# A two-block network in fp32 on one core: hi|lo products of the second MLP and of the SwiGLU side by side, and the order of the work changed in the attention, three norm boundaries and the gates

## The chip, the cores and the metric

The kernel runs on one core of a Trainium2 chip. The metric is the device time of one launch in microseconds (us). The kernel before takes 940.36 us (median of 3 runs, 940.02 to 941.78).

## The reference

256 tokens with 1024 features pass through two residual blocks, a final norm, and then a third block of another kind. All weights and activations are fp32. What matters here:

```python
for i in range(2):                       # first_block
    mod = silu(c) @ w_mod[i] + b_mod[i]
    sh1, sc1, g1, sh2, sc2, g2 = split(mod, 6)
    h = rmsnorm(x, norm_mix[i]) * (1 + sc1) + sh1
    y = pool_mixer(h) if i == 0 else moba_attention(h)
    x = x + g1 * y
    h = rmsnorm(x, norm_mlp[i]) * (1 + sc2) + sh2
    x = x + g2 * (relu(h @ w_up[i]) ** 2 @ w_down[i])   # w_up 1024 x 4096
...
h = concat(meta, rmsnorm(x, norm_final))  # second_block, 16 meta tokens ahead
proj = rmsnorm(h) @ w_in                  # gated deltanet + forgetting attention
h = h + concat(o_gdn, o_fox) @ w_out
f = rmsnorm(h)
h = h + (silu(f @ w_gate) * (f @ w_up)) @ w_down        # hidden width 2816
```

With 256 tokens the MoBA attention has a single key block: it is causal attention of 16 heads of 64 features with a relative-position bias.

## The kernel before, in words

**Products.** Every fp32 number that enters a matmul is held as two fp32r parts, hi (the rounded value) and lo (the rest). `mm3` (L261) makes one product out of three matmuls: hi·hi (L262), and the two mixed ones (L263, L264). A weight arrives in pieces of 128x1024 by DMA (queue of SP), its hi half is made on ACT (`piece_hi`, L245) and its lo half on DVE (`piece_lo`, L251); five such pairs can stand at once. With the weights stationary (`ws_steps`, L959) one tile of 128 output features and 256 tokens takes 8 k-steps of `mm3`, so 24 matmuls of 256 columns; with the tokens stationary (`tm_steps`, L970) the columns are 512 features.

**MLP and SwiGLU.** `mlp` (L1034) runs over 8 chunks of 512 hidden features. `up` (L1072) makes the four feature tiles of a chunk in two pairs, each pair in one PSUM bank of 512 columns; `split_act` (L1086) squares the relu and splits it into hi and lo for `dn`, the product with w_down (48 matmuls of 512 columns per chunk). Chunk 0 of MLP 1 (`up_first`, L1058) is made with tokens stationary and then transposed (`upt`), one half of the tokens after the other; it is followed by chunk 1's `up` and chunk 0's `dn`. In the SwiGLU `gate_up` (L1998, ten times) and `swi` (L1974) do the like for a chunk of 256 hidden features, with silu(gate) times up; the product with w_down there is `fd`.

**PSUM.** Eight banks: four for accumulators (`acc_tile`), two for products (`mm_tile`) and two for transposes (`tp_tile`).

**Boundaries.** `boundary` (L521) stands between a block half and the next: it adds the gated result to x (DVE), squares and sums (ACT), takes the reciprocal root (DVE), normalizes (`normalize`, L547), transposes on PE (8 matmuls per half of the tokens, `*_tp`), scales by the modulation (`scaled`, ACT) and splits into hi and lo (`split`, DVE, L395 and L396). Its order on ACT, DVE and PE is as written. Between the two token halves PE works on what is held back: `products(n)` takes n steps from the generator `ahead`, which are the previous section's last products (two `mm3`, six matmuls each) and, in two boundaries, then the next section's first products of 128 tokens. Boundary att1 leads into the attention, mlp1 into MLP 1, f into the SwiGLU. In mlp1 `R_HOLD` = 3 such steps come before the first transposes.

**Attention.** `attention` (L1138) writes PE's order by hand: a clock of estimated costs runs along the projections (`project`, `quarter_values`, `wo`), and a table of events with due times (`H_S`, `H_P`, `H_T`, `H_V` and so on) places, for each pair of heads, the scores, the softmax (`softmax_rows`, DVE L1115 to L1120 and ACT L1118), the transposes of P (`pt`) and the product P·V (`pv`). After each projection and each quarter of the values `riding` (L1182) lets one unit of another job go: two columns of the modulation (`wmc`, L444), that is a DMA of 1024 KB on SP and two row products of 128x1024 on DVE. There are ten such places, and the first six use the job up.

**Gates.** In the second block `interleave` (L111) mixes the deltanet's convolution products (`conv_proj`) with the gates' short chain (`early_gates`); `R_GATE` is how many steps of the chain follow each step of the products.

Everything else is ordered by the tile framework's scheduler. The few lines of the arithmetic that the change replaces:

```python
def mm3(ps, l, r, first, last):
    pe.matmul(ps, l[0], r[0], start=first, stop=False)
    pe.matmul(ps, l[0], r[1], start=False, stop=False)
    pe.matmul(ps, l[1], r[0], start=False, stop=last)
```

Of the kernel before, what the change touches and what calls it, by code (L numbers as in the profile page):

```python
# [36 lines left out]
R_GATE = 2.0  # L37
# [4 lines left out]
H_V = 2.0  # L42
H_TL = 5.0
DELAY = 3
C_FEAT = 0.6
# [5 lines left out]
R_HOLD = 3  # L51
# [59 lines left out]
def interleave(main, filler, ratio=None):  # L111

    owed = 0.0
    for r in main:
        owed += r if ratio is None else ratio
# [42 lines left out]
def build(tc, a, out):  # L158
# [4 lines left out]
    with ctx:  # L163
# [357 lines left out]
        def boundary(ac, gate, scale, shift, h, c0, name, ahead, final=None):  # L521
# [3 lines left out]
            with tc.manual_schedule(engines=VA | {mybir.EngineType.PE}):  # L525
# [80 lines left out]
                elif w is not None:  # L606
# [3 lines left out]
                    products(8)  # L610
# [8 lines left out]
                    w.piece_lo(3)  # L619
                    normalize(1)  # L620
                else:
# [347 lines left out]

        def tm_steps(w, h, tok0, m, ps, grain=2):  # L970
# [63 lines left out]
        def mlp(i, h, w0, wn, at, ahead=None):  # L1034


            def act2(src, name):
                n = src.shape[1]
                r = t2k(f"{name}r")[:, :n]
# [32 lines left out]
            def up(j):  # L1072
                w = ahead if i == 0 and j == NUP else split_chunk(a[f"w_up_{i}"][j - (1, NUP)[i == 0]], f"wu{i}{j}")
                ab = a_tile(j)
                for pr in range(2):
                    ps = mm_tile(f"up{i}{j}{pr}")
                    for q in range(2):
                        weights_stationary(w, h, 2 * pr + q, ps[:, q * S:(q + 1) * S])
# [59 lines left out]
        def attention(i, h, w0, wn):  # L1138
# [7 lines left out]
            st = {}  # L1146

# [34 lines left out]
            def riding():  # L1182
                ride(4)
# [158 lines left out]
        h = boundary(ac, lambda: gates[1, 0], *mods(1, 1), hl_tiles("mlp1", S), 0, "mlp1", (rest, wu1))  # L1342
# [783 lines left out]
```

## Time and profile before

| | |
|---|---|
| median of 3 runs | 940.36 us (940.02 to 941.78) |
| the profiled execution | 940.04 us |
| its span (first to last instruction) | 938.3 us |
| PE busy | 910.2 us (97%), 6045 matmuls |
| DVE busy | 638.0 us (68%) |
| ACT busy | 497.7 us (53%) |
| POOL busy | 12.5 us (1%) |
| DMA | 198.31 MB, mean 211 GB/s |
| mean granted PE clock | 0.995 |

The profile is that of one execution. PE is the engine of the matmuls, DVE the vector engine, ACT the scalar engine, POOL GpSimd, SP the engine that issues the DMAs. Matmuls overlap each other, so that one matmul's duration in a row is longer than the time from its start to the next one's start; the latter is called the cadence here and is what counts. A bracket behind a row gives the time for which the engine stood idle before it, and what released it.

### The profile page before, as it was taken

How to read it: one execution, taken by the hardware profiler on the slowest of the kernel's cores; microseconds unless marked ns; L12 is line 12 of the kernel's file. 1: busy time of each engine (PE TensorE's matmuls, PEld its weight loads, DVE VectorE, ACT ScalarE, POOL GpSimd, SP SyncE). 2: the span in 40 equal slices, each digit the busy share in tenths (PEclk: the TensorE clock that was granted, in tenths of full speed). 3: DMA queues.
4: the chain of work that ended last, by engine and by line, in shares of the span. 5: the costliest groups of instructions: out<-in, count | busy, mean ns of one | idle time of the engine just before them, and what ended most of it. 6: DMA issues, size and time to landing. Idle time of an engine off the chain costs nothing.

```text
span 938.3 us, 15294 instructions
## 1 busy us (share of the span) xinstructions
PE 910.2 (97%) x6045; PEld 794.0 (85%) x6045; DVE 638.0 (68%) x1222; ACT 497.7 (53%) x881; POOL 12.5 (1%) x22
## 2 busy tenths in 40 slices
PE   6999999999998999999999999999999999999996
PEld 3668889988797977889999978899988799999995
DVE  1686898878797775875556667797558765555544
ACT  4476444445556663744455555766456554444442
POOL 0000000000000000000000001000000000000000
PEclk9999999999999999999999999999999999999999
DMA  9998899889285560875565545332112555555531
GB/s 364 420 420 316 317 358 353 340 320 342 93 331 197 169 225 0 299 274 180 197 221 180 198 152 169 121 120 92 46 46 91 201 195 198 187 184 180 180 136 45
DMA packets 34555, 198.31 MB, mean 211 GB/s; under 512 B 4186, under 2 KB 6818, under 8 KB 14002
## 3 DMA queue, kind: packets, MB, share of 16 engines
q1 hardware_dynamic: 34338, 197.27, 59.0%
q8 instruction: 47, 0.77, 0.3%
q14 instruction: 24, 0.20, 0.1%
q10 hardware_dynamic: 146, 0.08, 0.0%
HBM read 196.24 MB, written 1.09 MB: 210 GB/s over the span
## 4 chain that ended last, share of the span: by engine, by line
PE 87%; DVE 5%; DMA 3%; ACT 2%; issue 2%; POOL 0%; DVEq 0%; POOLq 0%; ACTq 0%
PE up L262 7%; PE up L264 6%; PE up L263 6%; PE dn L262 6%; PE dn L264 6%; PE dn L263 6%; PE gu L264 4%; PE gu L263 4%; PE gu L262 4%; PE qk L291 2%; PE fd L262 2%; PE fd L263 2%; PE fd L264 2%; PE cp L264 1%; PE cp L262 1%
## 5 line engine op out<-in xcount | busy, mean ns | idle before, releaser
L262 PE MATMUL up<-mlp_hi,wu_h 128*128 128x256 f32 x416 | 118.5, 285 | 0.0
L264 PE MATMUL up<-mlp_hi,wu_l 128*128 128x256 f32 x416 | 117.7, 283 | 0.6 <-DVE wu_l L251 0.6
L263 PE MATMUL up<-mlp_lo,wu_h 128*128 128x256 f32 x416 | 117.9, 284 | 0.0
L245 ACT ACTIVATE wd_h<-wd_r 128x1024 fp32r<-128x1024 f32 x58 | 61.3, 1060 | 66.2 <-PE up L263 42.1
L245 ACT ACTIVATE wu_h<-wu_r 128x1024 fp32r<-128x1024 f32 x58 | 60.8, 1063 | 65.9 <-PE dn L264 48.8
L251 DVE TENSOR_TENSOR wu_l<-wu_r,wu_h 128x1024 fp32r<-128x1024 f32 x58 | 70.3, 1221 | 36.9 <-ACT wu_h L245 36.6
L251 DVE TENSOR_TENSOR wd_l<-wd_r,wd_h 128x1024 fp32r<-128x1024 f32 x58 | 70.7, 1222 | 35.4 <-ACT wd_h L245 34.9
L262 PE MATMUL dn<-wd_h,a 128*128 128x512 f32 x232 | 91.1, 393 | 0.0
L263 PE MATMUL dn<-wd_l,a 128*128 128x512 f32 x232 | 90.9, 392 | 0.0
L262 PE MATMUL gu<-f_hi,wgu_h 128*128 128x256 f32 x320 | 90.7, 283 | 0.0
L264 PE MATMUL gu<-f_hi,wgu_l 128*128 128x256 f32 x320 | 90.6, 283 | 0.0
L263 PE MATMUL gu<-f_lo,wgu_h 128*128 128x256 f32 x320 | 90.6, 283 | 0.0
L264 PE MATMUL dn<-wd_h,a 128*128 128x512 f32 x232 | 90.4, 390 | 0.0
L251 DVE TENSOR_TENSOR wgu_l<-wgu_r,wgu_h 128x1024 fp32r<-128x1024 f32 x44 | 53.6, 1224 | 51.3 <-ACT wgu_h L245 51.3
L262 PEld LDWEIGHTS up<-mlp_hi,wu_h 128*128 128x128 f32 x416 | 79.7, 192 | 1.0 <-issue 0.5
L263 PEld LDWEIGHTS up<-mlp_lo,wu_h 128*128 128x128 f32 x416 | 79.7, 192 | 1.0 <-issue 0.5
L264 PEld LDWEIGHTS up<-mlp_hi,wu_l 128*128 128x128 f32 x416 | 79.7, 192 | 0.8 <-DVE wu_l L251 0.8
L245 ACT ACTIVATE wgu_h<-wgu_r 128x1024 fp32r<-128x1024 f32 x44 | 46.6, 1062 | 62.0 <-PE gu L263 29.4
L263 PEld LDWEIGHTS gu<-f_lo,wgu_h 128*128 128x128 f32 x320 | 61.4, 192 | 0.3
L262 PEld LDWEIGHTS gu<-f_hi,wgu_h 128*128 128x128 f32 x320 | 61.4, 192 | 0.4
L264 PEld LDWEIGHTS gu<-f_hi,wgu_l 128*128 128x128 f32 x320 | 61.4, 192 | 0.0
L264 PEld LDWEIGHTS dn<-wd_h,a 128*128 128x128 f32 x232 | 43.6, 188 | 10.0 <-issue 0.9
(792 smaller groups left out, 2269.7 us busy)
## 6 DMA issues: line engine op xcount, KB each, us to landing
wu_r<-in_w_up_dram SPq DMA_DIRECT2D x32, 1024.0 KB, 5.2
wd_r<-in_w_down_dram SPq DMA_DIRECT2D x32, 1024.0 KB, 6.4
wgu_r<-in_w_gu_dram SPq DMA_DIRECT2D x22, 1024.0 KB, 5.2
wmc<-in_w_modc_dram SPq DMA_DIRECT2D x16, 1024.0 KB, 6.9
wmg<-in_w_modg_dram SPq DMA_DIRECT2D x12, 1024.0 KB, 6.8
wfd_r<-in_w_fd_dram SPq DMA_DIRECT2D x11, 1024.0 KB, 4.8
wi_r<-in_w_in_dram SPq DMA_DIRECT2D x10, 1024.0 KB, 5.1
wms<-in_w_mods_dram SPq DMA_DIRECT2D x16, 512.0 KB, 9.9
```

Of the source, the lines that this page charges most:

```text
L245: act.activation(hi, r, AF.Copy)
L251: vec.tensor_tensor(lo, r, hi.bitcast(F32), ALU.subtract)
L262: pe.matmul(ps, l[0], r[0], start=first, stop=False)
L263: pe.matmul(ps, l[0], r[1], start=False, stop=False)
L264: pe.matmul(ps, l[1], r[0], start=False, stop=last)
L291: f(*a, **k)
```

## The change

1. In MLP 1's `up` and in `gate_up`, h is laid out with hi and lo of a k-tile side by side (`hl_beside`, `Part`, `both`). `ws_halves` takes two matmuls per k-step in place of three: the weight's hi half times [hi|lo], 512 columns, and its lo half times hi, 256 columns into the first half of the bank. The bank's halves are then added: `halves_sum` is one ACT copy and one DVE add of 128x256 per feature tile. A tile takes a bank to itself, from `mm_tile` and `tp_tile` in turn (`halves_tile`). There are 7 chunks of 4 tiles in MLP 1 and 10 of 4 in the SwiGLU, with 8 k-steps each. The relu is then taken in place.
2. In boundary mlp1 `R_HOLD` is 4; the products ahead now go on into MLP 1's first ones (`up100`), six steps of them before the second transposes and two after.
3. In boundaries att1 and f the scalings of k-tiles 4 and 6 both stand before the last squares.
4. In the attention the first pair's transposes and P·V are due 1.5 later, the P·V of pair 5 at 3.5 in place of 2.0, the six units of the modulation ride at the 1st, 2nd, 3rd, 6th, 8th and 10th place (`RIDES`) in place of the first six, a one-element Exp (`exp_table`) is written before the third projection, and three steps of `wo` now follow the last P·V.
5. In the gates `R_GATE` is a list, and PE's order there is as written.

```diff
-R_GATE = 2.0
+R_GATE = (1.0, 2.0, 5.0, 2.0, 2.0, 3.0)
+H_VL = 3.5
+H_FIRST = 1.5
+RIDES = (1, 2, 3, 6, 8, 10)
-R_HOLD = 3
+R_HOLD = 4
...
+        def ws_halves(w, h, ft, ps):
+            p2 = ps.rearrange("p (e n) -> p e n", e=2)
+            for kt in range(KT):
+                wl = w(ft * PIECE + kt * P, P)
+                pe.matmul(p2, wl[0], both(h, kt, slice(0, S)), start=kt == 0, stop=False)
+                pe.matmul(p2[:, 0], wl[1], h[0][:, kt], start=False, stop=kt == KT - 1)
+        def halves_tile(q, name):
+            return (mm_tile, tp_tile)[q](name)
+        def halves_sum(dst, ps):
+            act.activation(dst, ps[:, S:], AF.Copy)
+            vec.tensor_tensor(dst, ps[:, :S], dst, ALU.add)
...
                     products(R_HOLD)
                     w.piece_hi(2)
                     normalize(0)
-                    products(8)
+                    products(8 - R_HOLD)
...
                     w.piece_lo(3)
+                    products(6)
                     normalize(1)
+                    products(2)
...
-                    hf = scaled(0, 4)
+                    hfs = [scaled(0, kt) for kt in (4, 6)]
                     squares(1, 1)
-                    split(hf, 0, 4)
+                    split(hfs[0], 0, 4)
                     products(2)
-                    hf = scaled(0, 6)
-                    normalize(1, lambda: split(hf, 0, 6))
+                    normalize(1, lambda: split(hfs[1], 0, 6))
...
             def riding():
-                ride(4)
+                rode[0] += 1
+                if rode[0] in RIDES:
+                    ride(4)
...
+                lag += H_FIRST if pr == 0 else 0.0
...
-                           (at + lag + by + H_V, hd + 1, pv, pr)]
+                           (at + lag + by + (H_V, H_VL)[pr == 5], hd + 1, pv, pr)]
...
+            act.activation(work.tile([P, 1], F32, tag="psum", name="exp_table", bufs=4), ones[:, 0:1], AF.Exp)
...
-            for k in range(4):
-                until_head(9 + 2 * k)
-                next(steps)
-            next(steps, None)
+            for hd in (9, 11, 13):
+                until_head(hd)
+                if hd < 13:
+                    next(steps)
+            until_head(15)
+            for _ in range(3):
+                next(steps, None)
```

**What moves on the engines: DVE at the first softmax.** These are DVE's instructions around the first pair of heads' softmax in the attention. `sm` are the scores of a head (L1115 adds the bias and takes the maxima; `sm_nm` is the negated maximum that ACT's Exp waits for, `sm_rs` the reciprocal of the sum), `wqk_l` is a lo half of a weight piece, `wmc` a column of the modulation. Before:

```order
L444 ISA wmc_2795,modcol_103<-wmc_2795,crow,vecs 128x1024
L444 ISA modcol_103 128x1
...
L251 TENSOR_TENSOR wqk_l_2893<-wqk_r_2801,wqk_h_2892 128x1024
L448 SCALAR_TENSOR_TENSOR modcol_103<-modcol_103,vecs 128x1
L1117 TENSOR_SCALAR sm_nm<-sm_m 128x1 x3
L444 ISA wmc_2927,modcol_103<-wmc_2927,crow,vecs 128x1024
L444 ISA modcol_103 128x1
L444 ISA wmc_2927,modcol_103<-wmc_2927,crow,vecs 128x1024
L444 ISA modcol_103 128x1
L251 TENSOR_TENSOR wqk_l_2936<-wqk_r_2933,wqk_h_2935 128x1024
```

With the change:

```order
L254 TENSOR_TENSOR wqk_l_2801<-wqk_r_2798,wqk_h_2800 128x1024
L1172 ISA sm_2599,sm_m<-s_2591,toep_2589 128x128
L1172 ISA sm_m 128x1
...
L1174 TENSOR_SCALAR sm_nm<-sm_m 128x1 x3
L254 TENSOR_TENSOR wqk_l_2883<-wqk_r_2798,wqk_h_2882 128x1024
L1174 TENSOR_SCALAR sm_nm<-sm_m 128x1
L1176 RECIPROCAL sm_rs<-sm_s 128x1 x3
L1177 TENSOR_SCALAR sm_2599<-sm_2599,sm_rs 128x128
L1177 TENSOR_SCALAR sm_2599<-sm_2599,sm_rs 128x256
L1177 TENSOR_SCALAR sm_2618<-sm_2618,sm_rs 128x128
L254 TENSOR_TENSOR wqk_l_2928<-wqk_r_2925,wqk_h_2927 128x1024
```

The two modulation columns (`wmc`, four long instructions with their accumulator reads) that stood before the scores and between the negated maxima and what follows are gone from this place; two `wqk_l` remain around the chain. On PE, 18 more matmuls `qk` stand before the first transposes `pt`.

**PE in chunk 0 of MLP 1.** `up110` and `up111` are chunk 1's feature tiles, `upt101` the transposes of chunk 0's second token half, `dn` chunk 0's product with w_down. `wu11_h0` to `h3` are chunk 1's weight pieces, one for each tile. Before, all of `up110` and `up111` (96 matmuls) come before the first `dn`:

```order
L262 MATMUL up111_4020<-mlp1_hi_3699,wu11_h3_4051 128x256
L263 MATMUL up111_4020<-mlp1_lo_3700,wu11_h3_4051 128x256
L264 MATMUL up111_4020<-mlp1_hi_3699,wu11_l3_4052 128x256
L262 MATMUL dn100_3943<-wd10_h0_4099,a10_3870 128x512
L263 MATMUL dn100_3943<-wd10_l0_4100,a10_3870 128x512
L264 MATMUL dn100_3943<-wd10_h0_4099,a10_3870 128x512
L262 MATMUL dn101_3944<-wd10_h0_4099,a10_3870 128x512
L263 MATMUL dn101_3944<-wd10_l0_4100,a10_3870 128x512
L264 MATMUL dn101_3944<-wd10_h0_4099,a10_3870 128x512
```

With the change:

```order
L1005 MATMUL up1100_3951<-mlp1_1_3702,wu11_l0_3955 128x256
L1098 MATMUL upt100_3902<-ident_85,up100q_3900 128x128 x4
L1004 MATMUL up1110_4012<-mlp1_0_3701,wu11_h2_4015 128x512
...
L1005 MATMUL up1110_4012<-mlp1_1_3702,wu11_l2_4016 128x256
L1098 MATMUL upt101_3938<-ident_85,up101q_3936 128x128 x4
L265 MATMUL dn100_3945<-wd10_h0_4079,a10_3897 128x512
L266 MATMUL dn100_3945<-wd10_l0_4080,a10_3897 128x512
L265 MATMUL dn101_3946<-wd10_h0_4079,a10_3897 128x512
L266 MATMUL dn101_3946<-wd10_l0_4080,a10_3897 128x512
L1004 MATMUL up1101_3976<-mlp1_0_3701,wu11_h1_3977 128x512
L1005 MATMUL up1101_3976<-mlp1_0_3701,wu11_l1_3978 128x256
```

The second tile that PE takes is now `up1110`, out of chunk 1's third weight piece; the tile `up1101` of the second weight piece stands behind `upt101` and four matmuls of `dn`.

**ACT's tables.** `ACT_TABLE_LOAD` is the load of an activation function's table. Before, around the first softmax:

```order
L1179 ACTIVATE att_k<-qk_2503 128x512
L245 ACTIVATE wqk_h_2892<-wqk_r_2801 128x1024
L245 ACTIVATE wqk_h_2935<-wqk_r_2933 128x1024
L1179 ACTIVATE att_q<-qk_2568 128x512
L1118 ACT_TABLE_LOAD
L1118 ACTIVATE sm_2597,sm_s<-sm_2597,sm_nm 128x128
L1118 ACTIVATE sm_2597,sm_s<-sm_2597,sm_nm 128x256
```

With the change, at the start of the program and then at the same softmax:

```order
L1350 ACT_TABLE_LOAD
L1350 ACTIVATE exp_table<-ones 128x1
L346 ACTIVATE n_sq_117,n_ss<-x 128x512
...
L1237 ACTIVATE att_k<-qk_2503 128x512
L248 ACTIVATE wqk_h_2882<-wqk_r_2798 128x1024
L1175 ACT_TABLE_LOAD
L1175 ACTIVATE sm_2599,sm_s<-sm_2599,sm_nm 128x128
```

`exp_table` stands at the very start of ACT's order, ahead of the first squares, and the load before the first softmax's Exp is still there, one `wqk_h` and the copy `att_q` earlier than before.

## Rows read from the trace of the kernel before

**Rows 1.** The page: busy time by engine, then the chain that ended last, by engine.

```profile
PE 910.2 (97%) x6045; PEld 794.0 (85%) x6045; DVE 638.0 (68%) x1222; ACT 497.7 (53%) x881; POOL 12.5 (1%) x22
...
PE 87%; DVE 5%; DMA 3%; ACT 2%; issue 2%; POOL 0%; DVEq 0%; POOLq 0%; ACTq 0%
```

**Rows 2.** Timeline of PE, one chunk of MLP 1: start us, us, operation [idle before].

```profile
432.16 0.28 PE L262 MATMUL up<-mlp_hi,wu_h 128*128 128x256 f32 x1
...
443.67 0.40 PE L262 MATMUL dn<-wd_h,a 128*128 128x512 f32 x1
...
454.58 0.28 PE L262 MATMUL up<-mlp_hi,wu_h 128*128 128x256 f32 x1
```

**Rows 3.** Windows: stretch, length, busy us (instructions) per engine, PE clock, DMA share, GB/s.

```profile
432.16:454.58 22.42, 22.42 (x145) 20.53 (x144) 11.89 (x12) 10.72 (x12) 0.00 (x0) 1.00 0.58 188
382.00:400.00 18.00, 18.00 (x128) 16.91 (x127) 17.51 (x22) 12.58 (x18) 0.00 (x0) 1.00 0.99 355
```

**Rows 4.** Timeline of ACT, first SwiGLU chunks: 128x256 out of PSUM.

```profile
818.33 0.36 ACT L1977 ACTIVATE sg<-gu 128x256 f32<-128x256 f32 x1
```

**Rows 5.** Timeline of DVE, the same stretch: 128x256 out of PSUM.

```profile
819.60 0.41 DVE L1978 TENSOR_TENSOR sg<-sg,gu 128x256 f32<-128x256 f32 x1
```

**Rows 6.** Timeline of PE, attention, around the first softmax.

```profile
282.48 0.28 PE L291 MATMUL qk<-att_hi,wqk_l 128*128 128x256 f32 x1
...
286.32 1.08 PE L291 MATMUL pt<-ident,sm 128*128 128x128 f32 x3 [3.56 <-DVE sm_nm L1117]
...
294.70 0.93 PE L291 MATMUL s<-att_k,att_q 64*128 64x128 f32 x8
```

**Rows 7.** Windows of the same stretch: the granted clock.

```profile
286.00:288.00 2.00, 1.56 (x7) 1.38 (x8) 2.00 (x10) 1.48 (x5) 0.00 (x0) 0.72 1.09 387
288.00:290.00 2.00, 2.00 (x12) 2.00 (x11) 2.00 (x11) 0.72 (x3) 0.00 (x0) 0.50 0.93 379
```

**Rows 8.** Timeline of DVE, the same stretch.

```profile
279.89 1.27 DVE L444 CUSTOM_DVE_ANT_0 wmc<-wmc,crow,vecs 128x1024 f32<-128x1024 f32 x1
...
282.30 1.21 DVE L251 TENSOR_TENSOR wqk_l<-wqk_r,wqk_h 128x1024 fp32r<-128x1024 f32 x1
...
284.52 1.21 DVE L251 TENSOR_TENSOR wqk_l<-wqk_r,wqk_h 128x1024 fp32r<-128x1024 f32 x1
```

**Rows 9.** Timeline of ACT, the same stretch.

```profile
280.31 1.28 ACT L1118 ACT_TABLE_LOAD   x1
```

**Rows 10.** Timeline of PE, end of attention: products P·V.

```profile
338.86 0.65 PE L291 MATMUL pv<-pT,att_v 128*64 128x256 f32 x2
...
340.67 0.86 PE L291 MATMUL pv<-pT,att_v 128*64 128x256 f32 x6 [1.16 <-ACT pT L1218]
...
341.47 0.38 PE L291 MATMUL v<-wv_h,att_hi 128*128 128x256 f32 x1
...
349.58 0.87 PE L291 MATMUL pv<-pT,att_v 128*64 128x256 f32 x8
...
355.34 1.58 PE L291 MATMUL pv<-pT,att_v 128*64 128x256 f32 x8
...
357.39 0.50 PE L291 MATMUL wo<-wo_h,att_o_hi 128*128 128x512 f32 x1 [0.47 <-ACT att_o_hi L982]
```

**Rows 11.** Timeline of PE: transposes in boundaries (att1, then mlp1 twice).

```profile
252.46 1.06 PE L566 MATMUL att_tp<-ident,att_xn 128*128 128x128 f32 x8 [1.28 <-DVE att_xn L562]
...
363.84 1.09 PE L566 MATMUL mlp_tp<-ident,mlp_xn 128*128 128x128 f32 x8 [0.69 <-DVE mlp_xn L562]
...
377.17 1.03 PE L566 MATMUL mlp_tp<-ident,mlp_xn 128*128 128x128 f32 x8
...
379.04 0.50 PE L262 MATMUL up<-wu_m,mlp_hi 128*128 128x512 f32 x1 [0.84 <-DVE mlp_hi L395]
```

**Rows 12.** Timeline of ACT, boundary mlp1.

```profile
375.60 0.72 ACT L563 ACTIVATE mlp_xn<-x,mlp_y 128x512 f32<-128x512 f32 x1 [1.54 <-DVE mlp_y L320]
```

**Rows 13.** Timeline of PE, gates of the second block.

```profile
587.39 0.20 PE L1471 MATMUL fc<-masks,logf 16*8 16x16 f32 x2 [0.33 <-DVE logf L1464]
```

More of the change, by code (lines that the diff above doesn't have):

```diff
@@ L108, with interleave @@
 V_BG, V_POOL = 15, 16
-def interleave(main, filler, ratio=None):
+def interleave(main, filler, ratios):
     owed = 0.0
-    for r in main:
-        owed += r if ratio is None else ratio
+    for n, _ in enumerate(main):
+        owed += ratios[n]
         while owed >= 1.0:
@@ L401, in modulated_group, with __init__, __getitem__ @@
                 pair_split(pair_scaled(tp, scale, shift, kt, name, rows), hi, lo, c0, kt, rows)
+        class Part:
+            def __init__(self, tiles, e):
+                self.tiles, self.e = tiles, e
+            def __getitem__(self, at):
+                p, k, *c = at
+                c = c[0] if c else slice(None)
+                if isinstance(k, slice):
+                    g = k.start // 4
+                    k = slice(k.start - 4 * g, k.stop - 4 * g)
+                else:
+                    g, k = k // 4, k % 4
+                return self.tiles[g][p, k, self.e, c]
         def hl_tiles(name, n):
@@ L406, in hl_tiles, with hl_beside, both @@
             return hi, lo
+        def hl_beside(name, n):
+            tiles = [big_tile(f"{name}_{g}", F32R)[:, :KT * n].rearrange("p (k e n) -> p k e n", k=4, e=2) for g in range(2)]
+            return Part(tiles, 0), Part(tiles, 1)
+        def both(h, kt, cols):
+            return h[0].tiles[kt // 4][:, kt % 4, :, cols]
         p1ctx = ExitStack()
@@ L1075, in up @@
                 for pr in range(2):
[L1076 removed]
+                    sums = t2k(f"up{i}{j}{pr}s") if i else mm_tile(f"up{i}{j}{pr}")
                     for q in range(2):
[L1078 removed]
+                        if not i:
+                            weights_stationary(w, h, 2 * pr + q, sums[:, q * S:(q + 1) * S])
+                            if q:
+                                ride(R_LEFT)
+                                if j >= R_FROM:
+                                    ride(R_LEFT)
+                            continue
+                        ps = halves_tile(q, f"up{i}{j}{pr}{q}")
+                        ws_halves(w, h, 2 * pr + q, ps)
+                        halves_sum(sums[:, q * S:(q + 1) * S], ps)
                         if q:
@@ L1341, in build @@
             ride(4)
-        h = boundary(ac, lambda: gates[1, 0], *mods(1, 1), hl_tiles("mlp1", S), 0, "mlp1", (rest, wu1))
+        h = hl_beside("mlp1", S)
+        boundary(ac, lambda: gates[1, 0], *mods(1, 1), h, 0, "mlp1", (ahead(rest, wu1, h, "up100"), wu1))
         def wide_row(src, name):
@@ L1899, in early_gates @@
                 gdn_decays(i)
-        interleave(urgent(early_gates()), conv_proj(1, gk, 1), R_GATE)
+        with tc.manual_schedule(engines={mybir.EngineType.PE}):
+            interleave(urgent(early_gates()), conv_proj(1, gk, 1), R_GATE)
         def rounds(fill, *gens):
@@ L1976, in swi @@
             sg = t4("tmp", name, 6).rearrange("p h n -> p (h n)")
-            act.activation(sg[:, :S], ps[:, :S], AF.Silu)
-            vec.tensor_tensor(sg[:, S:], sg[:, :S], ps[:, S:], ALU.mult)
+            if len(ps) == 1:
+                act.activation(sg[:, :S], ps[0][:, :S], AF.Silu)
+                vec.tensor_tensor(sg[:, S:], sg[:, :S], ps[0][:, S:], ALU.mult)
+            else:
+                for q in range(2):
+                    halves_sum(sg[:, q * S:(q + 1) * S], ps[q])
+                act.activation(sg[:, :S], sg[:, :S], AF.Silu)
+                vec.tensor_tensor(sg[:, S:], sg[:, :S], sg[:, S:], ALU.mult)
             return sg[:, S:]
@@ L2001, in gate_up @@
             for ft in range(2):
-                ps = mm_tile(f"gu{j}{ft}")
+                ps = [halves_tile(q, f"gu{j}{ft}{q}") for q in range(2)]
                 for q in range(2):
-                    weights_stationary(w, fh, 2 * ft + q, ps[:, q * S:(q + 1) * S])
+                    ws_halves(w, fh, 2 * ft + q, ps[q])
                 split_to(ab[:, 0, ft], ab[:, 1, ft], swi(ps, f"sg{j}{ft}"))
```

23 lines of the change are left out of this document (14 added, 9 removed).

## Prediction

> **What bounds the kernel now.** I read the page first: PE is busy 97% of the span and makes up 87% of the chain that ended last, with DVE next at 5% [rows 1]. The mean granted clock is 0.995, so nearly always the higher level. So time can go in two ways only: PE gets less to do, or one of its few idle stretches goes. Then I read the timeline of PE for the cadence and for its idle brackets, and at each bracket the timelines of DVE and ACT for what the releaser had been behind.
>
> The cadence: 96 `up` matmuls of 256 columns take 443.67 − 432.16 = 11.51 us, 0.1199 each; the 48 `dn` of 512 columns after them take 10.91 us, 0.2273 each [rows 2]. Two of 256 cost 0.2398, one of 512 costs 0.0125 less: a matmul has a fixed part on top of its columns.
>
> **Term 1, the halves side by side.** Per k-step and tile, three matmuls of 256 (0.3597) become one of 512 and one of 256 (0.2273 + 0.1199 = 0.3472): −0.0125 us. There are 7×4×8 = 224 places in MLP 1 and 10×4×8 = 320 in the SwiGLU: −2.8 and −4.0 us. This takes the two cadences, measured in runs of one kind, as holding when the kinds alternate; that is the assumption. The ends: nothing, if alternating costs the fixed part again, and 6.8.
> What it adds: one ACT copy and one DVE add per tile. The nearest rows are 0.36 us [rows 4] and 0.41 us [rows 5]. Per chunk of MLP 1 that is 4×0.36 = 1.4 us more on ACT, busy 10.7 of 22.4, and 4×0.41 = 1.6 on DVE, busy 11.9 [rows 3]. Both keep 40% free, so I cost it at nothing in the steady chunks. The chain of a tile grows by about 0.8 us before `dn` can use it, but `dn` begins with the chunk's first two tiles, 5.5 us of work at its cadence, and this covers the last two. Were ACT and DVE full, each tile would show that 0.8 us.
>
> **Term 2, the first softmax.** PE's last `qk` starts at 282.48, the first `pt` at 286.32 [rows 6]: 3.84, less one cadence of 0.12, so 3.72 us lost. The releaser is DVE's `sm_nm`; DVE is full there (4.00 of 4.00 us from 286 to 290 [rows 7]), and its row products `wmc` (1.27 each) and lo halves `wqk_l` (1.21 each) stand between the pieces of the softmax chain [rows 8], while ACT loads a table for 1.28 us [rows 9]. Then PE runs at a granted clock of 0.72 and of 0.50, the 1.2 GHz level, for some 4 us [rows 7]: from 286.32 to 294.70 [rows 6] are 8.38 us for 48 `qk` (48×0.12 = 5.76) and two sets of three transposes (eight take about 1.05 with their drain [rows 11], so a set some 0.35): 1.9 us lost. Together 5.6 us.
> With the change the first `pt` stands 18 `qk` later (18×0.12 = 2.2 us), and on DVE four row products (4×1.2 = 4.9 us) no longer stand around the chain. 4.9 + 2.2 = 7.1 us of room against a wait of 3.7: I take the whole 5.6 as gained. The six units of `wmc` aren't fewer, two of them come later with their 1024 KB each on SP's queue, at places where DVE has gaps. What is late next is the second pair's softmax, by the order behind two `wqk_l`, a `wmc` unit and a `wv_l` on DVE; I see a slack of some half a microsecond, so the lower end of this term is 2.
> `exp_table` I cost at nothing. In the order it has drifted to the start of the program, and the table load before the first softmax is still there: as a warm-up it does not do what it says. The load stays at 1.28 us in the chain; it merely comes earlier because `wqk_h` and `att_q` no longer stand ahead of it.
>
> **Term 3, the end of the attention.** A P·V of eight matmuls takes about 0.8 us where nothing holds it (0.87 with its drain) [rows 10]. The one at 338.86 takes 341.47 − 338.86 = 2.61, so 1.8 too many, 1.16 of it idle for ACT's `pT`. With the due time moved by 1.5 it comes behind more products. But two P·V then stand closer together, and the second may wait for the same queue on ACT: between 0 and 1.3 us. I take 0.6, so −1.2. The last one takes 357.39 − 355.34 = 2.05, so 1.24 too many, of which 0.47 is the wait for `att_o_hi` [rows 10]. Twelve `wo` matmuls (2.8 us) now follow it and cover that part: −0.5; the wait for `pT` inside it stays.
>
> **Term 4, the boundaries.** In mlp1 PE is idle for 0.69 before the first transposes and for 0.84 after the second [rows 11]. Holding six more matmuls (1.4 us) covers the first; six `up100` matmuls after the second transposes cover the second. But the second transposes come six matmuls, 1.4 us, sooner in PE's order. ACT's half of `mlp_xn` ends at 376.32 [rows 12], 0.85 us before they start at 377.17, so some 0.5 us of new wait is left there; and the drains around both waits go too (0.2 to 0.3). Sum −1.3, ends −0.5 and −1.7.
> In att1 1.28 us of idle precede the second transposes [rows 11]. One lo half of a split (0.41, the same form as in [rows 5]) no longer stands in the way of the root's chain: −0.4. Boundary f has the same edit; no wait of size is there, nothing.
>
> **Term 5, chunk 0 of MLP 1.** This goes the other way. The tile in the transposes' bank must wait until `upt100` is split, and so PE's order now puts four `dn` matmuls, then the tile `up1101`, behind `upt101`. The first needs DVE for `a`'s lo half, and DVE is busy 17.5 of the 18 us from 382 to 400 [rows 3] with lo halves of 1.2 us (as in [rows 8]). So `up1101` should wait for about one queued piece less what PE has ahead, 0.8 us, and `dn` for a weight's half queued behind it on ACT, 0.4: +1.2. Ends: 0, and three queued pieces, 3.6.
>
> **Term 6, gates.** `fc` waits 0.33 for `logf` [rows 13]; the chain is now issued two to five steps at a time early on, with PE in the written order: −0.3. At worst the chain's first matmuls wait on DVE about as long: 0.
>
> **Sum.** −2.8 −4.0 −5.6 −1.2 −0.5 −1.3 −0.4 +1.2 −0.3 = −14.9. On the profiled execution (940.04, of which 938.3 is span) that is 925.1; the median of the three runs stands 0.3 above it, so 925.4 us.
>
> The Trainium skill (TensorE: Matmul & The Clock Gate, section "Wait — 56ns, not 53.3ns?") states a fixed cost of about 2.5 ns per warm matmul; an estimate from it would make term 1 some 1.4 us in place of 6.8. The 12.5 ns per matmul of [rows 2] speak against it here.
>
> **Rivals.**
> A: the halves bring next to nothing. The fixed part shows in runs of equal matmuls; when a 256 follows a 512, the short one may leave too little time for the next weights, and each pair may pay its 0.0125 back. For it: nothing in the trace alternates these two kinds. Against it: runs of 256 hold 0.12 although each has its own weight load. Time: 925.4 + 6.8 = 932.2. Chance 0.14. The page of the Trainium skill just named leads near the same place, by its estimate to 925.4 + 5.4 = 930.8.
> B: the first softmax stays late. If DVE's remaining `wqk_l` still part the chain and PE idles long enough for the clock to fall again, 5.6 comes back: 931.0. For it: DVE is full from 286 to 290 [rows 7]. Against it: 7.1 us of room. Chance 0.10.
> C, slower: the sum of the halves becomes PE's wait. A bank is free only when ACT's copy and DVE's add are through, and both queue behind weight halves of about 1.2 us [rows 8]. There are 68 tiles; if each made PE wait as long as the copy and the add take, 0.77 us, this would be 52 us, and it decides from 14.9/68 = 0.22 us per tile. For it: ACT and DVE run in order, and two banks serve only transposes before. Against it: a bank's turn comes again after three other tiles, over 8 us later. At 0.36 us (the copy alone) per tile: 925.4 + 24.5 = 949.9. Chance 0.04.
> The forecast keeps 0.72.
>
> **How the numbers follow.** A measurement of this kernel can tell about 0.2%, 1.9 us. All cases but C end below 938.5: faster 0.94; C gives slower 0.04; small mixtures in between 0.02. The range: below, terms 3, 4 and 5 at their good ends (0.6, 0.4 and 1.2) and the chain in the gates somewhat better give 922.5, and stretches that I costed at nothing, some 2 us, 920.5; above it takes in A and B, each alone, up to 933.
>
> **What would show it.** PE's busy time falls by about 7 and its idle time by 8. In an MLP 1 chunk, `up` should take 64 matmuls in 11.1 us; 11.5 means A. The bracket before the first `pt` should be under 0.5 and the granted clock from 286 to 290 near 1; if not, B. Brackets at the first `up` matmul of each tile with ACT or DVE as releaser mean C. Between the mlp1 transposes and chunk 1's `dn` I expect brackets of about 0.5, 0.8 and 0.4. Wrong in size I would be first in terms 5 and 3, whose new waits no row of before shows.

## The result, and the profile after

The changed kernel takes 926.82 us (median of 4 runs, 924.60 to 927.82) against 940.98 us (940.02 to 941.78) for the kernel before in the same comparison: ratio 0.9847, 95% interval 0.9824 to 0.9870. Forecast were 925.4 us, with 920.5 to 933.0 as the range. The profiled execution took 927.82 us with a span of 926.0 us, 12.3 us less than the span before.

The page after, the same two lines as in [rows 1]: 544 matmuls fewer, PE busy 4.7 us less, its idle time (span less busy) 20.5 us where it was 28.1, and the chain a little more PE's own.

```profile
PE 905.5 (98%) x5501; PEld 764.2 (83%) x5501; DVE 661.3 (71%) x1290; ACT 517.5 (56%) x950; POOL 12.7 (1%) x22
...
PE 89%; DVE 4%; DMA 3%; issue 2%; ACT 1%; SPq 0%; POOL 0%; DVEq 0%; POOLq 0%; ACTq 0%
```

Timeline of PE, one chunk of the second MLP (start us, us, operation), to be read beside [rows 2]. The 64 `up` matmuls take 456.48 − 445.19 = 11.29 us, where 96 took 11.51 before, and `dn` 10.94 where it took 10.91.

```profile
445.19 0.39 PE L1004 MATMUL up<-mlp,wu_h 128*128 128x512 f32 x1
...
456.48 0.40 PE L265 MATMUL dn<-wd_h,a 128*128 128x512 f32 x1
...
467.42 0.39 PE L1004 MATMUL up<-mlp,wu_h 128*128 128x512 f32 x1
```

Timeline of PE at the first softmax, to be read beside [rows 6]: the first `pt` follows the last `qk` after 0.12 us, one cadence, without a bracket.

```profile
285.58 0.28 PE L294 MATMUL qk<-att_hi,wqk_l 128*128 128x256 f32 x1
...
285.70 0.49 PE L294 MATMUL pt<-ident,sm 128*128 128x128 f32 x3
```

Windows (stretch, length, busy us per engine, PE clock, DMA share, GB/s), the first two beside [rows 7], the others beside [rows 3]: the clock stays at 1.00 behind the first softmax, and DVE is busy 15.7 of 18 us in chunk 0 (17.5 before) and 13.2 of 22.2 in a later chunk. Chunk 0 comes about 9 us sooner here, so its 18 us begin at 373 and not at 382.

```profile
286.00:288.00 2.00, 2.00 (x19) 2.00 (x18) 2.00 (x4) 2.00 (x7) 0.00 (x0) 1.00 0.77 171
288.00:290.00 2.00, 2.00 (x18) 1.91 (x17) 2.00 (x7) 1.06 (x3) 0.00 (x0) 1.00 0.75 270
373.00:391.00 18.00, 18.00 (x96) 15.35 (x96) 15.71 (x20) 11.03 (x17) 0.00 (x0) 1.00 0.92 351
445.19:467.42 22.23, 22.23 (x114) 18.81 (x112) 13.21 (x16) 11.88 (x16) 0.00 (x0) 1.00 0.57 190
```

Timeline of PE at the end of the attention, beside [rows 10]. From its start to the next product, the P·V that took 2.61 us now takes 1.00 (the row at 336.79), the one behind it 1.04 in place of 0.80, and the last one 1.44 in place of 2.05.

```profile
336.79 0.87 PE L294 MATMUL pv<-pT,att_v 128*64 128x256 f32 x8
...
342.92 1.11 PE L294 MATMUL pv<-pT,att_v 128*64 128x256 f32 x8
...
347.52 1.51 PE L294 MATMUL pv<-pT,att_v 128*64 128x256 f32 x8
```

Timeline of PE, the boundaries and the gates, beside [rows 11, 13]: 0.91 is left of 1.28 in att1, nothing of 0.69 at the first transposes of mlp1, 0.28 is new before the second, and 0.82 us after these, without a bracket, PE goes on (1.87 before, of which 0.84 idle). The gates' `fc` waits for nothing.

```profile
253.41 1.06 PE L593 MATMUL att_tp<-ident,att_xn 128*128 128x128 f32 x8 [0.91 <-DVE att_xn L589]
...
357.26 1.03 PE L593 MATMUL mlp_tp<-ident,mlp_xn 128*128 128x128 f32 x8
...
368.20 1.06 PE L593 MATMUL mlp_tp<-ident,mlp_xn 128*128 128x128 f32 x8 [0.28 <-DVE mlp_xn L589]
...
369.02 0.48 PE L265 MATMUL up<-wu_h,mlp 128*128 128x512 f32 x1
...
573.98 0.20 PE L1539 MATMUL fc<-masks,logf 16*8 16x16 f32 x2
```

For the experiments, the stretches between the starts of certain matmuls are compared, in us: they are free of what happens in the program's start, which differs from run to run (last section). A stretch ends at the start of the matmul that is named, also where that matmul stands inside a merged row.

| stretch | before | changed, first run | changed, again |
|---|---|---|---|
| first v of att1 to first qk | 13.4 | 13.0 | 13.0 |
| first qk to first pt | 26.1 | 24.5 | 24.5 |
| first pt to first mlp transposes | 77.5 | 71.6 | 71.7 |
| to up100 | 7.8 | 6.3 | 6.3 |
| to the last up | 162.4 | 160.1 | 160.1 |
| to the first fvm | 21.9 | 21.9 | 21.9 |
| gates: to g0ktp | 49.8 | 50.0 | 50.0 |
| to the first gu | 136.1 | 136.1 | 136.0 |
| first to last gu | 177.2 | 175.0 | 175.0 |

Six `wo` matmuls (1.4 us) stand in the third row after and in the fourth before. From the first v product to the last matmul of the program it is 683.0 us before and 669.4 in both runs of the changed kernel: 13.5 us less. The third row is the least steady: it came out 0.7 and 1.2 us longer in two runs below that change nothing in it.

### The profile page after: what moved, and what is told of

It reads as the page before. It is cut to its first block, busy times and chain, and to the rows that moved or that the text cites. A ratio compares the mean times of both kernels' runs of the same rounds, so it can differ in the third digit from the quotient of the medians.

```text
span 926.0 us, 14378 instructions
## 1 busy us (share of the span) xinstructions
PE 905.5 (98%) x5501; PEld 764.2 (83%) x5501; DVE 661.3 (71%) x1290; ACT 517.5 (56%) x950; POOL 12.7 (1%) x22
## 4 chain that ended last, share of the span: by engine, by line
PE 89%; DVE 4%; DMA 3%; issue 2%; ACT 1%; SPq 0%; POOL 0%; DVEq 0%; POOLq 0%; ACTq 0%
PE gu L1004 8%; PE dn L267 6%; PE dn L265 6%; PE dn L266 6%; PE up L1004 6%; PE gu L1005 4%; PE qk L294 4%; PE up L265 4%; PE up L267 4%; PE up L266 3%; PE up L1005 3%; DMA wms<-in_w_mods_dram 2%; PE fd L265 2%; PE fd L267 2%; PE fd L266 2%
## 5 line engine op out<-in xcount | busy, mean ns | idle before, releaser
L1004 PE MATMUL gu<-f,wgu_h 128*128 128x512 f32 x320 | 113.5, 398 | 0.0
L248 ACT ACTIVATE wd_h<-wd_r 128x1024 fp32r<-128x1024 f32 x58 | 61.3, 1061 | 70.8 <-PE up L1004 28.1
L254 DVE TENSOR_TENSOR wu_l<-wu_r,wu_h 128x1024 fp32r<-128x1024 f32 x58 | 70.2, 1222 | 28.1 <-ACT wu_h L248 27.9
L1005 PE MATMUL gu<-f,wgu_l 128*128 128x256 f32 x320 | 89.8, 281 | 0.0
L1004 PE MATMUL up<-mlp,wu_h 128*128 128x512 f32 x224 | 79.3, 397 | 0.0
L1004 PEld LDWEIGHTS gu<-f,wgu_h 128*128 128x128 f32 x320 | 60.1, 188 | 14.7
L1005 PE MATMUL up<-mlp,wu_l 128*128 128x256 f32 x224 | 62.8, 280 | 0.0
L1005 PEld LDWEIGHTS gu<-f,wgu_l 128*128 128x128 f32 x320 | 60.4, 189 | 0.4
L265 PE MATMUL up<-mlp_hi,wu_h 128*128 128x256 f32 x192 | 55.2, 288 | 0.0
L267 PE MATMUL up<-mlp_hi,wu_l 128*128 128x256 f32 x192 | 54.3, 284 | 0.6 <-DVE wu_l L254 0.6
L266 PE MATMUL up<-mlp_lo,wu_h 128*128 128x256 f32 x192 | 54.3, 283 | 0.0
L266 PEld LDWEIGHTS dn<-wd_l,a 128*128 128x128 f32 x232 | 43.6, 188 | 9.3 <-issue 0.7
```

Of the source, the lines that this page charges most:

```text
L248: act.activation(hi, r, AF.Copy)
L254: vec.tensor_tensor(lo, r, hi.bitcast(F32), ALU.subtract)
L1004: pe.matmul(p2, wl[0], both(h, kt, slice(0, S)), start=kt == 0, stop=False)
L1005: pe.matmul(p2[:, 0], wl[1], h[0][:, kt], start=False, stop=kt == KT - 1)
```

## The experiments

All change the changed kernel, which ran again beside the first group as its base. They were measured in three groups; the kernel before ran in each and gave 940.80, 941.13 and 940.46 us.

**The base.**

> The changed kernel once more, beside the others of this group, as their base. Both theories: 926.8 us, within 1.5 of it. In its trace a chunk of the second MLP's up takes 11.29 us for 64 matmuls (0.3528 a place) in most chunks and the first 48 us are bound by the start's DMAs; if the clock dip between 48 and 64 us (0.79 in the first trace of the change, 0.89 before) is chance, the first v product (248.13 there, 246.82 before) will start at another time than 248.1.

927.09 us (924.47 to 929.63). Every stretch of the table came out within 0.2; only the start moved, the first v product from 248.13 to 247.34.

**Three matmuls again.**

```diff
-pe.matmul(p2, wl[0], both(h, kt, slice(0, S)), start=kt == 0, stop=False)
+pe.matmul(p2[:, 0], wl[0], h[0][:, kt], start=kt == 0, stop=False)
+pe.matmul(p2[:, 1], wl[0], h[1][:, kt], start=False, stop=False)
 pe.matmul(p2[:, 0], wl[1], h[0][:, kt], start=False, stop=kt == KT - 1)
```

> Three matmuls of 256 columns again in place of 512 + 256, all else of the change kept, the sums of the halves too. Theory 'cadence when the kinds alternate is 0.3528 a place': back to 3 x 0.1199 = 0.3597, so 544 x 0.0069 = 3.8 us slower than the changed kernel, 11.51 us a chunk, about 930.6. Rival 'the saving is the 6.8 us of the prediction and something else in these chunks eats 3 us': 6.8 slower, 933.6. Rival 'nothing': 926.8. ACT and DVE stay as they are, so brackets at tile starts, if any, stay too.

930.47 us. Timeline of PE, one chunk: 96 matmuls in 454.95 − 443.44 = 11.51 us.

```profile
443.44 0.28 PE L1004 MATMUL up<-mlp,wu_h 128*128 128x256 f32 x1
...
454.95 0.40 PE L265 MATMUL dn<-wd_h,a 128*128 128x512 f32 x1
```

The stretch to the last `up` is 161.85 (base 160.07), first to last `gu` 177.00 (175.04): 1.78 and 1.96 us more. The halves are worth 3.7 us, not 6.8 and not nothing. The sums stayed in, and yet first to last `gu` is no longer than before the change (177.17; the 0.17 between them is boundary f's, below): they cost PE nothing that shows.

**Not alternating.**

```diff
 for kt in range(KT):
     wl = w(ft * PIECE + kt * P, P)
     pe.matmul(p2, wl[0], both(h, kt, slice(0, S)), start=kt == 0, stop=False)
+for kt in range(KT):
+    wl = w(ft * PIECE + kt * P, P)
     pe.matmul(p2[:, 0], wl[1], h[0][:, kt], start=False, stop=kt == KT - 1)
```

> The same matmuls, but for each tile first the eight of 512 columns, then the eight of 256, so that the kinds no longer alternate. Theory 'alternating costs 0.0056 a place': 8 x 0.2273 + 8 x 0.1199 = 2.778 a tile, 11.11 us a chunk in place of 11.29, 17 chunks: 3.1 us faster than the changed kernel, 923.7. Rival 'the cadence depends on something else (what else reads the memory, or the two-part operand of 512)': 11.29 a chunk stays, 926.8.

925.77 us (923.44 to 926.86). Timeline of PE, one chunk: 64 matmuls in 454.93 − 443.79 = 11.14 us, in the others 11.15 to 11.18. Three quarters of the extra cost of alternating are gone, by the order alone.

```profile
443.79 1.98 PE L1004 MATMUL up<-mlp,wu_h 128*128 128x512 f32 x8
...
454.93 0.40 PE L265 MATMUL dn<-wd_h,a 128*128 128x512 f32 x1
```

The stretch to the last `up` is 159.4 (base 160.1) and first to last `gu` 173.4 (175.0): 0.7 and 1.6 us less, 2.3 of the 3.1 expected. The stretch behind the first pt was 72.5, 0.7 over the base, though nothing was changed there: one `pt` waits 1.16 us for DVE's `sm` that waited 0.52 in the base and not at all in the first run, and ACT had waited 2.0 us for a piece of w_o. It isn't only the time at which PE gets there: three matmuls back had its first v product at the same time (245.66 against 245.64) and no such wait. What sets it stays open.

**The riders back.**

```diff
-RIDES = (1, 2, 3, 6, 8, 10)
+RIDES = (1, 2, 3, 4, 5, 6)
```

> The modulation's units ride at the first six places again; the first transposes stay 1.5 later in the table. Theory 'the riders on DVE between the softmax's pieces made the wait': most of the 3.7 us wait returns less the 2.2 us by which PE comes later, so 1.5 to 3.7 us idle before the first pt, and 1 to 2 us more if the granted clock falls: 1.5 to 5.6 us slower, about 930. Rival 'the later due time alone removed the wait': no bracket over 0.5 before the first pt, 926.8.

928.00 us, and no wait before the first `pt` (0.12 us from the last `qk`). It is the rival that held. The stretch behind the first pt grew by 0.8 us (72.5), and the products P·V differ there: one takes, on the timeline of PE, 326.27 − 324.82 = 1.45 us, about 0.6 too many, and one at 342.64 takes 1.67 where it took 0.80 in the base, against one that takes 0.6 less. The first of these three took 1.35 us in the kernel before too, which no term priced.

```profile
324.82 1.53 PE L294 MATMUL pv<-pT,att_v 128*64 128x256 f32 x8
...
326.27 0.38 PE L294 MATMUL qk<-att_hi,wqk_h 128*128 128x256 f32 x1
```

**The first pair earlier.**

```diff
-H_FIRST = 1.5
+H_FIRST = 0.0
```

> The first pair's transposes due as early as before, the modulation's units at the changed places. Theory 'the later due time alone removed the first softmax's wait' (the run with the old places showed no bracket there): the first pt waits again, 2.2 us (the 18 qk that no longer stand before it) less the slack there was, so 1 to 2.2 us idle, with or without a fall of the clock: 1 to 4 us slower than the changed kernel, 928 to 931. Rival 'either of the two edits is enough': no bracket over 0.5, 927.

927.02 us. The rival again: the first `pt` comes 2.1 us sooner behind the first qk (22.4 us) and has no bracket, on the timeline of PE:

```profile
282.56 0.49 PE L294 MATMUL pt<-ident,sm 128*128 128x128 f32 x3
```

From the first qk to the mlp transposes it is 22.4 + 73.6 = 96.0; the two runs of the changed kernel have 96.1 and 96.3. So neither edit alone is needed.

**Both back.**

> Both edits at the first softmax taken back, the units at the first six places and the first pair due as before; the end of the attention stays changed. Theory 'either edit is enough, and only without both does the wait come back': 2 to 4 us idle before the first pt with DVE's sm_nm as releaser, a granted clock under 0.9 behind it, and the stretch from the first qk to the first mlp transposes (96.2 us in the changed kernel) 4 to 6 us longer: about 931.5. Rival 'it was the other edits of the attention': no bracket, 927.

932.66 us. Timeline of PE, then windows of the same stretch: 3.03 us idle for `sm_nm`, and the lower clock behind it.

```profile
274.33 0.93 PE L294 MATMUL s<-att_k,att_q 64*128 64x128 f32 x8 [1.01 <-ACT att_k L1237]
...
283.41 0.28 PE L294 MATMUL qk<-att_hi,wqk_l 128*128 128x256 f32 x1
...
286.72 1.13 PE L294 MATMUL pt<-ident,sm 128*128 128x128 f32 x3 [3.03 <-DVE sm_nm L1174]
...
294.87 0.93 PE L294 MATMUL s<-att_k,att_q 64*128 64x128 f32 x8
```

```profile
286.00:288.00 2.00, 1.28 (x5) 1.02 (x6) 2.00 (x9) 1.12 (x5) 0.00 (x0) 0.66 1.03 370
288.00:290.00 2.00, 2.00 (x12) 2.00 (x11) 2.00 (x8) 0.70 (x3) 0.00 (x0) 0.50 0.97 379
```

From the first qk to the mlp transposes it is 26.5 + 76.0 = 102.5, 6.2 more than the base. Either edit is enough and only without both does the wait of before come back, with its fall of the clock. Not all of the 6.2 is the softmax's: the first pair's scores waited 1.0 us for ACT's `att_k`. Reckoned as the prediction did it for the kernel before, the wait is 286.72 − 283.41 − 0.12 = 3.2 us and the clock behind it 294.87 − 286.72 less the 6.46 that 48 `qk` and two sets of `pt` take at full clock = 1.7, together 4.9.

Why the later due time alone was enough can be read from DVE. Its timeline in this run, and then in the run with only the riders back: here one unit of the modulation (two `wmc`, 2.4 us) runs between the negated maxima and what follows them; there one unit stands before the scores (275.15 and 276.36), and the next comes only behind the first `pt` (285.13). So the later due time also moved two row products out of the chain.

```profile
280.05 1.28 DVE L471 CUSTOM_DVE_ANT_0 wmc<-wmc,crow,vecs 128x1024 f32<-128x1024 f32 x1
...
281.26 1.28 DVE L471 CUSTOM_DVE_ANT_0 wmc<-wmc,crow,vecs 128x1024 f32<-128x1024 f32 x1
```

```profile
276.36 1.28 DVE L471 CUSTOM_DVE_ANT_0 wmc<-wmc,crow,vecs 128x1024 f32<-128x1024 f32 x1
...
286.44 1.27 DVE L471 CUSTOM_DVE_ANT_0 wmc<-wmc,crow,vecs 128x1024 f32<-128x1024 f32 x1
```

**No warm-up.**

```diff
-act.activation(work.tile([P, 1], F32, tag="psum", name="exp_table", bufs=4), ones[:, 0:1], AF.Exp)
```

> Without the one-element Exp; nothing else moves on ACT, DVE or PE but a table load at the very start, which goes back to the first square. Theory 'the warm-up does nothing': within 1 us of the changed kernel, the stages from the first v product on equal to 0.2 us, the table load before the first softmax still there. Rival 'a load at the start delays the first stage': the first v product about 1 us sooner than the 245.6 to 248.1 of the runs so far.

926.69 us, every stretch within 0.4 of the base. The Exp does nothing. The timeline of ACT in the changed kernel shows why it is harmless too: it runs at the very start, where before the first square's table was loaded at the same moment (1.68 us) and ACT then waited 1.79 us for x.

```profile
1.69 1.28 ACT L1350 ACT_TABLE_LOAD   x1 [1.69 <-PEq L2183]
...
2.98 0.20 ACT L1350 ACTIVATE exp_table<-ones 128x1 f32<-128x1 f32 x1
```

**The end of the attention back.**

```diff
-(at + lag + by + (H_V, H_VL)[pr == 5], hd + 1, pv, pr)]
+(at + lag + by + H_V, hd + 1, pv, pr)]
...
-            for hd in (9, 11, 13):
-                until_head(hd)
-                if hd < 13:
-                    next(steps)
-            until_head(15)
-            for _ in range(3):
-                next(steps, None)
+            for k in range(4):
+                until_head(9 + 2 * k)
+                next(steps)
+            next(steps, None)
```

> The P.V of pair 5 due as before and the last wo steps placed as before. Theory of the prediction: 1.2 + 0.5 us come back, the stretch from the first pt to the first mlp transposes (71.6 us in the changed kernel) is 1.5 to 2 longer, 928.5. Rival 'this stretch waits for the wo pieces' DMA whatever the order': less than 0.5 longer, 927.

927.59 us, in a run with an early start; from the first pt to the mlp transposes 73.7, 1.9 and 2.1 over the two runs of the changed kernel. Timeline of PE: both waits of before are there again, 1.31 for `pT` and 0.47 for `att_o_hi`.

```profile
333.32 0.86 PE L294 MATMUL pv<-pT,att_v 128*64 128x256 f32 x6 [1.31 <-ACT pT L1278]
...
347.98 1.52 PE L294 MATMUL pv<-pT,att_v 128*64 128x256 f32 x8
...
349.97 0.50 PE L294 MATMUL wo<-wo_h,att_o_hi 128*128 128x512 f32 x1 [0.47 <-ACT att_o_hi L1026]
```

**Boundary mlp1 back.**

```diff
-R_HOLD = 4
+R_HOLD = 3
...
-                    products(6)
+                    products(8)
                     normalize(1)
-                    products(2)
```

> Boundary mlp1 with three steps held and all of up100 before the second transposes, as before. Theory: 0.69 and 0.84 us of idle return, less the 0.28 that the change left before the second transposes: from the first mlp transposes less their held work to the end of chunk 0, 1.3 us longer, 928.2. Rival: the wait moves on into chunk 0 (DVE full there) and was not gained in full: under 0.6 us.

928.64 us. From the first pt to the last `up` 239.4 us, the base 238.1: 1.3 us. Timeline of PE, the first and the second wait:

```profile
355.68 1.09 PE L593 MATMUL mlp_tp<-ident,mlp_xn 128*128 128x128 f32 x8 [0.73 <-DVE mlp_xn L589]
...
370.88 0.50 PE L265 MATMUL up<-wu_m,mlp 128*128 128x512 f32 x1 [0.84 <-DVE mlp L398]
```

**Three small edits back.**

```diff
-        with tc.manual_schedule(engines={mybir.EngineType.PE}):
-            interleave(urgent(early_gates()), conv_proj(1, gk, 1), R_GATE)
+        interleave(urgent(early_gates()), conv_proj(1, gk, 1), R_GATE)
-R_GATE = (1.0, 2.0, 5.0, 2.0, 2.0, 3.0)
+R_GATE = (2.0, 2.0, 2.0, 2.0, 2.0, 2.0)
...
-                    hfs = [scaled(0, kt) for kt in (4, 6)]
+                    hf = scaled(0, 4)
```

> Three small edits taken back whose stages lie apart: the gates' list and PE's written order there, and the scalings in boundaries att1 and f. Theory: att1's stage (first v to first qk, 13.0 in the changed kernel) 0.4 longer, boundary f (between g0ktp and the first gu, 136.0 to 136.1) 0.1 to 0.2 longer, and the gates' stage (first fvm to g0ktp, 50.0) the same within 0.2, since the wait of 0.33 that the list took away came back in the small matmuls' switches. Rival of the prediction: the gates' stage 0.3 longer.

928.35 us, with the latest start of all (first v at 249.4). att1's stretch is 13.4 (base 13.0): the scalings there are worth 0.4. Boundary f's second transposes stand behind the first `gu`, so its edit shows in first to last `gu`, 175.2 (175.0), and on the timeline of PE: the wait for `f_xn` is 0.37 as before the change, and 0.20 in the changed kernel.

```profile
738.36 0.85 PE L593 MATMUL f_tp<-ident,f_xn 128*128 128x128 f32 x6 [0.37 <-DVE f_xn L589]
```

The gates' stretch is 50.1 (50.0): `fc` waits 0.33 for `logf` again (at 579.18), and only 0.1 of it shows.

**A faster version, and one step too far.** The first keeps the first chunk of the second MLP alternating (`j > 1` groups) and groups all others; the second also takes the halves into the first MLP, by the same `hl_beside` and `halves_sum`.

> The grouped order of c2_grouped, but not in the first chunk of the second MLP, where the wait for the lo half (1.6 us) took the gain. Theory: 11.15 in place of 11.29 a chunk and 0.04 less in what follows it, 16 chunks, so 2.5 to 2.9 us faster than the changed kernel: 924.2. Rival 'the stage behind the attention waits for DMA anyway': same stages, time lost in the attention as in c2_grouped, 925 to 926.

924.43 us (923.69 to 925.26), ratio to before 0.9830 (0.9817 to 0.9844), the fastest of all. The wait of 1.6 us that the expectation speaks of isn't one: in the trace of `c2_grouped` eight long matmuls stand in one row there. So the exception for the first chunk was not needed; to the last `up` it is 159.5 us here and 159.4 there. Timeline of PE, a chunk: 455.83 − 444.68 = 11.15 us.

```profile
444.68 1.98 PE L1009 MATMUL up<-mlp,wu_h 128*128 128x512 f32 x8
...
455.83 0.40 PE L265 MATMUL dn<-wd_h,a 128*128 128x512 f32 x1
```

The six stretches from up100 to the last matmul add up to 551.1 us, the base's to 553.8: 2.7 us, as between the medians. Of these, 2.2 stand in the stretches of the halves, and 0.2 in the one behind the first fvm, where nothing was changed.

> The same, and the halves side by side in the first MLP as well, six more chunks. Theory 'the matmul's fixed part alone': 6 x 0.36 = 2.2 us faster than f1_grouped, 922. Rival 'DVE is full there (92% busy) and the added sums make PE wait, or the DMA at 95% sets the pace': no gain or slower, 924 to 930, with brackets at up whose releaser is DVE or a DMA.

933.48 us, 9 slower than the last. PE waits once for 3.83 us, for DVE's `a` of the last chunk, and then stands at the lower clock for 6 us (timeline of PE, then windows):

```profile
242.62 0.79 PE L265 MATMUL dn<-wd_p,a 128*128 128x512 f32 x1 [3.83 <-DVE a L1149]
```

```profile
242.00:244.00 2.00, 1.38 (x3) 1.16 (x4) 1.26 (x3) 0.00 (x0) 0.00 (x0) 0.50 0.72 188
244.00:246.00 2.00, 2.00 (x6) 1.55 (x5) 0.00 (x0) 0.00 (x0) 0.00 (x0) 0.50 0.94 360
246.00:248.00 2.00, 2.00 (x6) 1.52 (x6) 0.69 (x1) 0.00 (x0) 0.00 (x0) 0.50 0.21 86
```

The wait and half of the 6 us at half the clock make 6.8 of the 7.4 us by which the first v comes later than in the version above (255.05 against 247.62; both runs had 0.89 as the start's clock), and the first transposes of att1 wait 1.3 us that they didn't there. The gain per chunk is there all the same: the 64 `up` of a whole chunk take 11.14 us (121.61 to 132.76), where 96 take 11.51 in the version above. What eats it is the order at the end, where the last tile's chain queues three times behind halves of the attention's weights: its sum on DVE until 237.81 us, its square on ACT until 240.69, `a` on DVE until 242.14. DVE wasn't full there (4.4 busy of the 6 us from 236). The rest of the 9 us, 1.3, stands behind the first pt, where a P·V waits 0.98 for `pT`.

## Why the prediction was right

The size came out by the mechanisms named. One gain was taken nearly twice too large, one cost hardly came, and these two errors go against each other: that the sum lies so near is in part luck.

| term | predicted | measured | by |
|---|---|---|---|
| 1 halves | −6.8 | −3.7 | three matmuls back |
| 2 first softmax | −5.6 | −4.9 to −6.2 | both edits back |
| 3 end of the attention | −1.7 | −2.0 | end back |
| 4 boundary mlp1 | −1.3 | −1.3 | mlp1 back |
| 4 boundary att1 | −0.4 | −0.4 | three small edits back |
| 4 boundary f | 0 | −0.2 | three small edits back |
| 5 chunk 0 | +1.2 | +0.1 | mlp1 back, against the kernel before |
| 6 gates | −0.3 | −0.1 | three small edits back |
| sum | −14.9 | −12.5 to −13.8 | stretches: −13.5; medians: −14.2 |

The interval of the ratio allows 12 to 17 us, so the medians can't check the sum closer than that; the stretches do, without the start. Both signs named in advance came: PE's idle time fell by 7.6 us (8 were expected), its busy time by 4.7 (7), and what is short there is term 1.

**Term 1** is the term that was mis-sized: "This takes the two cadences, measured in runs of one kind, as holding when the kinds alternate". They don't hold: a place takes 11.29/32 = 0.3528, not 0.3472. Rival A, that each pair pays its gain back, was nearly half right: 0.0056 of the 0.0125 is paid back, and grouping returns 0.0044 of it. That ACT's copies and DVE's adds cost nothing was right, and rival C never came near: behind the second mlp transposes PE shows one bracket in all, 0.20 in boundary f, and none at an `up` or a `gu`.

**Term 2** was right in price, place and mechanism: the wait and the clock behind it both returned in one run. But the reasoning gave the two edits 4.9 and 2.2 us of room against 3.7, so that the second could not have done it alone, and each alone removed the bracket. The count left out that the later due time also moves DVE's order: with the riders back, one of the two units stands behind the first `pt`, and 2.2 + 2.4 = 4.6 us cover the 3.7. This is read from the rows of these runs; no run keeps that unit in its place with the later due time.

**Terms 3 and 4** held within 0.3. The P·V behind the moved one lost 0.24 us in the first run (1.04 in place of 0.80), where 0.6 was priced. In mlp1 the new wait before the second transposes was 0.28 in place of some 0.5. Boundary f was put at nothing, for want of a wait of size; a wait of 0.37 was there, and 0.17 of it went.

**Term 5** priced waits that did not come. Between 350 and 400 us PE has one idle bracket in the base run, the 0.28 of the second transposes. What is left is about 0.1 us at the switches between `up` and `dn`: the first four `dn` take 1.01 us (0.91 at the cadence), the next 18 take 4.09, just the cadence. The stretches say the same: with boundary mlp1 back, second MLP and boundary take 168.5 us from the first mlp transposes to the last `up`, before the change 170.2; the 1.7 less are the 1.8 of the halves there and 0.1 lost. The premise that failed is DVE's share of before (17.5 of 18 us), taken as the share after: it was 15.7, since work had moved out of that stretch. Between the second mlp transposes and chunk 2, DVE has 8 `macc` instructions, a job of the modulation, where there were 13 (5.7 us in place of 9.2). That no wait came for this reason is read from rows and was not tried apart.

**Term 6** saw the wait of 0.33 go, and it went; but only 0.1 of it shows. From the first gate matmul (`small`) to g0ktp it is 32.28 us before and with the edit back, and 32.17 with it. Which of the small matmuls took back the 0.2 was not tried apart. That the whole stretch is longer (50.0 against 49.8 before) lies ahead of the gates, at its first `fvm` and `u_tp`, which take 0.2 us more in the changed kernel and also with the edit back; in the grouped versions they don't, and why stays open.

The warm-up does nothing, as the order of the instructions had told. Of the range, the lower end rests on 2 us for stretches costed at nothing and on 0.7 in the gates, which no row carried; of these the experiments show boundary f's 0.2.

## What to carry to other kernels

Price a matmul by the cadence of the mixture in which it will stand: the saving of merging two matmuls was half of what runs of one kind promised, and most of the other half came back by putting equal matmuls next to each other. Two edits at one wait are to be undone one by one and together; undone singly, both looked worthless here. Work added where DVE and ACT have room costs PE nothing that shows, but it has to be priced by what stands ahead of it in their queues: in the first MLP the last piece made PE wait 3.8 us. An idle PE of 3 to 4 us then cost half as much again in clock at the softmax (3.7 and 1.9 us before, 3.2 and 1.7 with both edits back) and, as an estimate, up to 3 us on 3.8 in the first MLP.

## What the runs showed of the hardware that was not expected

**A matmul's fixed part depends on its neighbours.** Runs of 256 columns take 0.1199 each, runs of 512 take 0.2273 [rows 2]; alternating, the pair takes 0.3528, 5.6 ns over the sum, and grouped by eights 11.15/32 = 0.3484. So the neighbours matter, but they aren't all: one chunk alone, the second regular one of the second MLP, alternates at 11.10 us in both runs of the changed kernel (423.20 to 434.30 in the first), all other whole ones at 11.28 to 11.30. The starts of its matmuls repeat after two pairs, those of the others after three; what sets this stays open. The Trainium skill (TensorE: Matmul & The Clock Gate, section "Wait — 56ns, not 53.3ns?") states about 2.5 ns of fixed cost for each warm matmul, on top of its columns at 2.4 GHz. By this 256 columns are 0.1067 us without the fixed cost, an estimate; the rows here show 13 ns more, and 16 ns when alternating, and the measurement decides.

**The start takes one of several lengths.** Between 48 and 64 us the granted clock was 1.00, 0.89 or 0.79, and the first v product of att1 came with it: at 245.6 to 245.7 us in the three traces with 1.00, 246.8 to 247.6 in the eight with 0.89, 248.1 and 249.4 in the two with 0.79 (the version with halves in the first MLP left out). The three below have 245.7, 247.3 and 248.1 us (windows, one row for each of the three: three matmuls back, the base, the changed kernel's first run).

```profile
48.00:64.00 16.00, 14.07 (x88) 8.67 (x88) 14.77 (x33) 11.53 (x22) 0.70 (x1) 1.00 1.02 421
```

```profile
48.00:64.00 16.00, 14.07 (x83) 8.15 (x81) 14.67 (x30) 11.40 (x22) 0.70 (x1) 0.89 1.02 421
```

```profile
48.00:64.00 16.00, 14.14 (x73) 7.84 (x72) 13.93 (x29) 10.28 (x21) 0.70 (x1) 0.79 1.02 421
```

PE isn't full there and the DMAs are; whether the clock makes the start longer or only goes with it is not shown. Runs of one kernel differ by as much (924.47 to 929.63 us in the base, with a mean granted clock of 0.998 in the fastest and 0.994 in the slowest), but one run of each was traced, so that this is the start again is likely and not shown. It is why the stretches above, not single times, carry the small terms. It also means that the first profile of the change shows 1.3 us less gain than the kernels differ by in their stretches.
